# A decoder step on one core: the row blocks of the conditioning, one at a time or in twos

## The chip, the cores and the metric

One NeuronCore of a Trainium2 chip runs the whole program. The metric is the device time of one execution in microseconds. It was 1034.29 us for the kernel before (median of 3 runs, 1033.81 to 1036.57).

## The reference

One layer of a hybrid decoder over 512 prompt tokens and 8 single-token samples (520 columns together), width 1024, all in float32:

```python
cs = silu(c)                                   # 1 prompt and 8 sample vectors
mod = cs @ w_mod + b_mod                       # 9 x 6144: sh1, sc1, g1, sh2, sc2, g2
h = rmsnorm(x, norm1_g) * (1 + sc1) + sh1
u = h @ w_in                                   # q, f, i, o-gate; x, y; ga, gb (8 x 1024 columns)
o_a = HGRN2 recurrence of q, f, i, normed, times silu(o-gate)
o_b = RG-LRU recurrence of conv(x), times gelu(y)
merged = sigmoid(ga) * (o_a @ w_branch_a) + sigmoid(gb) * (o_b @ w_branch_b)
x = x + g1 * (merged @ w_out)
h2 = rmsnorm(x, norm2_g) * (1 + sc2) + sh2
x = x + g2 * (square(relu(h2 @ w_ff1)) @ w_ff2)
y = rmsnorm(x, final_norm_g)                   # and the new recurrent states
```

The change concerns the line `mod`. Its six parts of 1024 columns are numbered 0 to 5 (sh1, sc1, g1, sh2, sc2, g2). Parts 1 and 0 are computed at the start; parts 2, 4, 3 and 5, in this order, are computed in the tail of the mixer, between the tiles of other products.

## The kernel before, in words

Activations lie transposed, 128 features by 520 columns, in 8 slices. Every large product is made tile by tile: a weight tile of 1024 x 128 is loaded by SP into one of the four buffers `wst` (L102), split by ACT into a rounded high part `whi` (L111) and by DVE into the rest `wlo` (L114), and `gemm` runs 48 matmuls at L150: for each of 8 slices whi times the high and the low part of the activation and wlo times the high part, each in two halves of 260 columns. The results go to one of two PSUM tiles `mm`, and ACT or DVE reads them from there.

The conditioning is computed in **row blocks**: 128 rows of `w_mod` by the 1024 columns of one part, 512 KB, loaded by SP at L100 into the same four `wst` buffers, and used as they are. `mod_rows` (L408) runs four matmuls with the same 128 x 32 stationary tile `cT`, each for 256 columns and each into other 32 partitions of one PSUM tile `pt`. Eight row blocks make a part. Then ACT copies the sums out (`modev`, L413), and `mod_cols` (L422) transposes them by matmuls into `modT`; it is issued by the next `gemm` at its last slice (`MODK`).

The order of the work is a list of steps in `run`; each names the weights that it takes. In the tail it has the 8 tiles of gate ga, the 8 tiles of w_branch_a, then gate gb and w_branch_b tile by tile in turn, and then the 8 tiles of w_out and the MLP. `mod_step` puts the row blocks between them: one after each of the last four ga tiles, two after each of the first four w_branch_a tiles, one after each of the other four, and one after each of the 16 tiles of the last loop, 32 in all.

`weights` makes from the list the order of the loads. A row block gets the threshold of the tile before its step, a tile that of the tile two before it (`AHEAD`), and `ready_w` issues loads up to three entries (`LOADS`) ahead of the entry that is taken. A buffer of a tile is free when DVE has split it, a buffer of a row block when TensorE has read it. SP issues its transfers in order; one that waits for its buffer holds those behind it. At the beginning of the tail, POOL loads the results of both recurrences from DRAM, 16 slices in two tags of buffers (L877, L882), and ACT and DVE split them into `a` and `b` (L200, L201); x itself is loaded and transposed (L924, L927) for the output projection.

A scheduler with a model of the times then orders the instructions of each engine; it may set a few matmuls of one step between those of another.

Of the kernel before, what the change touches and what calls it, by code (L numbers as in the profile page):

```python
# [20 lines left out]
KO = D // 128  # L21
# [6 lines left out]
TAIL = 3  # L28
# [47 lines left out]
class Kernel:  # L76
# [355 lines left out]

    def mod(self, part, k):

        w = self.take_w(self.mod_key(part, k))
        if k == 0:
            self.psm = self.ppt.tile([128, 512], F32, name="pt")
        self.mod_rows(self.psm, k, w)
        if k == KO - 1:
            self.mod_open = part, self.modT[:, 8 * part:8 * part + 8], self.mod_out(self.psm), \  # L440
                self.n2g if part == 4 else None

# [1106 lines left out]
    def run(self):  # L1549
        tc, i, enter = self.tc, self.i, self.ctx.enter_context  # L1550
        self.consts = enter(tc.tile_pool(name="consts", bufs=1))
        self.dram = enter(tc.tile_pool(name="dram", bufs=1, space=DRAM))
        self.sm = enter(tc.tile_pool(name="sm", bufs=2))
        self.wst = enter(tc.tile_pool(name="wst", bufs=WST))
        self.ma = enter(tc.tile_pool(name="ma", bufs=8))
        self.ppt = enter(tc.tile_pool(name="ppt", bufs=1, space=PSUM))
        self.ppb = enter(tc.tile_pool(name="ppb", bufs=1, space=PSUM))
        self.pmm = enter(tc.tile_pool(name="pmm", bufs=2, space=PSUM))
        self.pps = enter(tc.tile_pool(name="pps", bufs=2, space=PSUM))
        self.whl = enter(tc.tile_pool(name="whl", bufs=2))  # L1560
        self.act = enter(tc.tile_pool(name="act", bufs=2))
        self.early = ExitStack()
        self.hc = self.early.enter_context(tc.tile_pool(name="hc", bufs=1))
        self.ogs = self.hc.tile([128, H, NB], F32, name="ogs")
        self.os = self.hc.tile([128, H, NB], F32, name="os")
        self.xlast = self.hc.tile([128, KO, 11], F32, name="xlast")
        self.hlast = self.hc.tile([128, KO, 9], F32, name="hlast")
        self.oaT_d = self.dram.tile([H, 128, L], F32, name="oaT_d")
        self.obT_d = self.dram.tile([KO, 128, T], F32, name="obT_d")
        self.oa, self.ob, self.merged = [], [], []  # L1570

        win = i["w_in"][0]
        steps = []
        one = lambda name, m, fn, *a: steps.append(([(i[name][0], 0, m * 128)], fn, *a))
        mods = [(p, k) for p in (2, 4, 3, 5) for k in range(KO)]

        def mod_step(n=1):
            for _ in range(n):
                if mods:
                    p, k = mods.pop(0)  # L1580
                    steps.append(([self.mod_key(p, k)], self.mod, p, k))

        ga, gb = {}, {}
        self.rg = {}

        for h in range(H):
            kf, kq, kv, kg = self.head_cols(h)
            steps.append(([kf, kq, kg, kv][FIRSTS if h == 0 else 0:], self.head_start if h == 0 else self.head, h))
            for n in (h - 1, h) if h % 2 else (h, h + 1):
                one("w_in", (40 if h % 2 else 32) + n, self.rg_y if h % 2 else self.rg_x, n)  # L1590
        for m in range(KO):
            one("w_in", 48 + m, lambda m: ga.update({m: self.gate(6, m, self.slot(self.ma, "ma"))}), m)
            if m == TAIL:
                steps.append(([], self.end_recurrences))
                steps.append(([], self.begin_tail))
            if m > TAIL:
                mod_step()
        for m in range(KO):
            if m == 2:
                steps.append(([], self.rg_out))  # L1600
            one("w_branch_a", m, lambda m: self.branch("w_branch_a", m, self.oa, ga[m]), m)
            mod_step(2 if m <= TAIL else 1)
        for m in range(KO):
            one("w_in", 56 + m, lambda m: gb.update({m: self.gate(7, m, self.slot(self.tail, "t"))}), m)
            mod_step()
            one("w_branch_b", m, lambda m: self.merge(m, gb.pop(m), ga.pop(m)), m)
            mod_step()
        steps.append(([], self.load_xT))
        steps.append(([], self.shifts))
        steps.append(([], self.begin_strassen))  # L1610
        for m in range(KO):
            one("w_out", m, self.out_proj, m)
        steps.append(([], self.norm2))
        self.entries, self.use = self.plan()
        steps.append((self.entries[:FIRST], self.mlp))

        keys = [k for st in steps for k in st[0]]
        self.mlp_at = len(keys) - FIRST
        self.weights(keys)
        self.begin()  # L1620
        for _, fn, *a in steps:
            fn(*a)
# [250 lines left out]
```

## Time and profile before

| what | value |
|---|---|
| timed runs, median (lowest to highest) | 1034.29 us (1033.81 to 1036.57) |
| profiled execution, first to last instruction | 1032.9 us |
| mean granted TensorE clock | 0.997 |
| PE busy, share of the span | 98% |
| DVE, ACT, POOL busy | 67%, 50%, 12% |
| HBM read, written | 123.61 MB, 11.26 MB |

The trace gives the start of each instruction from the span's start. For TensorE the starts are measured and the ends modelled, so costs between products are read from start to start. A matmul in float32 shows as two records. Idle time of an engine counts only where it delays the engine that sets the end. The tail's row blocks lie between 438.7 and 615.0 us.

### The profile page before, as it was taken

What the parts mean: (1) busy time and instruction counts of PE and PEld (TensorE: products, weight loads), DVE (VectorE), ACT (ScalarE), POOL (GpSimd) and SP (SyncE); (2) the same over time, 40 slices, a digit from 0 to 9 for tenths busy, and PEclk for the clock granted to TensorE, in tenths of its full rate; (3) what the DMA queues carried; (4) which work ended last, traced back from release to release, by engine and by line L of the source; (5) the groups of instructions that cost most, each with busy time, mean ns of one, the idle gap of its engine ahead of it and who ended that gap; (6) DMA issues with size and microseconds to landing.
All of it is one profiled execution on the core that took longest, in us unless ns stands there. A gap on an engine that the chain in (4) does not pass through costs nothing. (4 is left out here: it accounts for less than half of the span.)

```text
span 1032.9 us, 23726 instructions
## 1 busy us (share of the span) xinstructions
PE 1008.7 (98%) x9756; PEld 967.5 (94%) x9756; DVE 691.4 (67%) x1520; ACT 520.8 (50%) x988; POOL 123.1 (12%) x228
## 2 busy tenths in 40 slices
PE   5999999999999999999999999999999999999997
PEld 2899999999999999988999999999999999999996
DVE  6787769595867869264233347667776776777685
ACT  4555744663575366342122235466555655655663
POOL 3200000000000000031000001011422231232140
PEclk9999999999999999999999999999999999999998
DMA  9673443434334324397555568322672474274242
GB/s 324 220 200 111 119 126 118 121 116 126 109 114 126 114 85 135 105 329 238 164 163 162 158 179 240 99 84 63 133 173 81 95 173 124 49 160 99 63 82 84
DMA packets 201822, 143.68 MB, mean 139 GB/s; under 512 B 6766, under 2 KB 189702, under 8 KB 201706
## 3 DMA queue, kind: packets, MB, share of 16 engines
q1 hardware_dynamic: 191090, 128.08, 41.6%
q0 software_dynamic: 10608, 14.05, 7.0%
q8 instruction: 76, 1.25, 0.5%
q14 instruction: 32, 0.26, 0.1%
q10 hardware_dynamic: 16, 0.03, 0.0%
HBM read 123.61 MB, written 11.26 MB: 131 GB/s over the span
## 5 line engine op out<-in xcount | busy, mean ns | idle before, releaser
L150 PE MATMUL mm<-h,whi 128*128 128x260 f32 (+1 forms) x2944 | 490.3, 286 | 0.0
L150 PEld LDWEIGHTS mm<-h,whi 128*128 128x128 f32 x2944 | 409.7, 189 | 5.2 <-issue 4.1
L150 PE MATMUL mm<-h,wlo 128*128 128x260 f32 x1472 | 305.2, 286 | 0.1
L111 ACT CAST whi<-wst 128x1024 fp32r<-128x1024 f32 x164 | 171.7, 1048 | 221.6 <-PE mm L150 182.0
L114 DVE TENSOR_TENSOR wlo<-wst,whi 128x1024 fp32r<-128x1024 f32 x164 | 200.3, 1223 | 102.0 <-ACT whi L111 100.3
L150 PEld LDWEIGHTS mm<-h,wlo 128*128 128x128 f32 x1472 | 230.5, 189 | 1.9 <-issue 0.8
L150 PE MATMUL mm<-a,whi 128*128 128x260 f32 x512 | 85.3, 286 | 0.0
L150 PEld LDWEIGHTS mm<-a,whi 128*128 128x128 f32 x512 | 70.5, 188 | 3.8 <-issue 3.3
L150 PE MATMUL mm<-a,wlo 128*128 128x260 f32 x256 | 51.7, 283 | 0.0
L877 POOL DMA_DIRECT2D t<-oaT_d x8 | 4.4, 552 | 387.8 <-ACT sq L750 378.1
L1270 DVE TENSOR_TENSOR f<-f 128x260 f32<-128x260 f32 x64 | 27.4, 428 | 27.6 <-ACT f L1265 26.9
L1259 ACT ACTIVATE ft<-ft,fsh 128x512 f32<-128x512 f32 (+2 forms) x36 | 24.0, 675 | 36.1 <-DVE ft L1256 36.1
L150 PE MATMUL mm<-b,whi 128*128 128x260 f32 x256 | 41.9, 286 | 0.0
L1262 POOL TENSOR_TENSOR ft<-ft,fsh 128x8 f32<-128x8 f32 x28 | 18.4, 657 | 187.3 <-DVE ft L1256 187.3
L150 PEld LDWEIGHTS mm<-a,wlo 128*128 128x128 f32 x256 | 39.5, 188 | 0.0
L150 PEld LDWEIGHTS mm<-b,whi 128*128 128x128 f32 x256 | 35.0, 188 | 3.3 <-issue 2.5
L1304 POOL DMA_DIRECT2D ma<-snap x28 | 26.8, 972 | 38.3 <-issue 29.2
L1286 POOL DMA_DIRECT2D ma<-snap x28 | 25.9, 926 | 36.7 <-DMA ma<-snap 25.1
L893 DVE TENSOR_TENSOR t<-mm,t 128x520 f32<-128x520 f32 x8 | 5.6, 700 | 36.5 <-PE mm L150 36.5
L1265 ACT ACTIVATE f<-ft 128x520 f32<-128x520 f32 (+1 forms) x36 | 20.7, 587 | 15.0 <-POOL ft L1263 13.0
L602 ACT ACTIVATE st<-st,fkq 128x128 f32<-128x128 f32 x64 | 20.2, 391 | 14.8 <-DVE fkq L581 12.5
L150 PE MATMUL mm<-b,wlo 128*128 128x260 f32 x128 | 25.9, 284 | 0.0
(579 smaller groups left out, 1940.9 us busy)
## 6 DMA issues: line engine op xcount, KB each, us to landing
wst<-in_w_in_dram SPq DMA_DIRECT2D x64, 512.0 KB
wst<-in_w_mod_dram SPq DMA_DIRECT2D x32, 512.0 KB
wst<-in_w_ff_dram SPq DMA_DIRECT2D x64, 256.0 KB
wst<-in_w_ff_dram SPq DMA_DIRECT2D x32, 512.0 KB
wm<-in_w_mod_dram SPq DMA_DIRECT2D x16, 512.0 KB
st<-in_state_hgrn_dram SPq DMA_DIRECT2D x8, 512.0 KB
vb<-vd SPq DMA_DIRECT2D x8, 512.0 KB
out_dram<-st SPq DMA_DIRECT2D x8, 512.0 KB
```

What stands on the lines that cost most here:

```text
L111: ins = self.nc.scalar.copy(hi, st)
L114: self.nc.vector.tensor_tensor(lo, st, hi.bitcast(F32), OP.subtract)
L150: self.last_product = self.nc.tensor.matmul(ps[s][:, :c.stop - c.start], x, y[:, c], start=first and n == 0, stop=last and n == 2)
L602: nc.scalar.activation(st[:, b], st[:, b], AF.Copy, scale=fkq[:, 0, b:b + 1])
L877: nc.gpsimd.dma_start(t[:, :L], self.oaT_d[h])
L893: self.nc.vector.tensor_tensor(self.two(s), ps, self.two(s), OP.mult)
L1259: nc.scalar.activation(t[:, :p], t[:, :p], AF.Relu, bias=sh[:, 0:1])
L1262: eng.tensor_tensor(t[:, p:], t[:, p:], sh[:, 1:9], OP.add)
L1265: nc.scalar.activation(f, self.two(self.ft)[:, a:a + n], AF.Square)
L1270: self.nc.vector.tensor_tensor(f[:, n], f[:, a], f[:, b], op)
L1286: nc.gpsimd.dma_start(x[1][:, b], v[:, :n], accum_op=OP.add)
L1304: nc.gpsimd.dma_start(x[t][:, a], s[p], accum_op=OP.add)
```

## The change

The row blocks are taken two at a time. `mod` takes the weights of blocks k and k + 1 and runs both, one behind the other; the part is closed after block 6 and 7. `mod_step` adds one such step. The steps stand after the ga tiles 5 and 7, after the w_branch_a tiles 0 to 3, 5 and 7, and after each w_branch_b tile: 16 steps of two blocks. The work, the loads and their sizes are the same, and so are the buffers.

```diff
     def mod(self, part, k):
 
-        w = self.take_w(self.mod_key(part, k))
+        w = [self.take_w(self.mod_key(part, k + n)) for n in range(2)]
         if k == 0:
             self.psm = self.ppt.tile([128, 512], F32, name="pt")
-        self.mod_rows(self.psm, k, w)
-        if k == KO - 1:
+        for n in range(2):
+            self.mod_rows(self.psm, k + n, w[n])
+        if k == KO - 2:
             self.mod_open = part, self.modT[:, 8 * part:8 * part + 8], self.mod_out(self.psm), \
                 self.n2g if part == 4 else None
...
-        mods = [(p, k) for p in (2, 4, 3, 5) for k in range(KO)]
-
-        def mod_step(n=1):
-            for _ in range(n):
-                if mods:
-                    p, k = mods.pop(0)
-                    steps.append(([self.mod_key(p, k)], self.mod, p, k))
+        mods = [(p, k) for p in (2, 4, 3, 5) for k in range(0, KO, 2)]
+
+        def mod_step():
+            p, k = mods.pop(0)
+            steps.append(([self.mod_key(p, k + n) for n in range(2)], self.mod, p, k))
...
-            if m > TAIL:
+            if m > TAIL and m % 2:
                 mod_step()
         for m in range(KO):
             if m == 2:
                 steps.append(([], self.rg_out))
             one("w_branch_a", m, lambda m: self.branch("w_branch_a", m, self.oa, ga[m]), m)
-            mod_step(2 if m <= TAIL else 1)
+            if m <= TAIL or m % 2:
+                mod_step()
         for m in range(KO):
             one("w_in", 56 + m, lambda m: gb.update({m: self.gate(7, m, self.slot(self.tail, "t"))}), m)
-            mod_step()
             one("w_branch_b", m, lambda m: self.merge(m, gb.pop(m), ga.pop(m)), m)
             mod_step()
```

## The prediction

> **What bounds the kernel now.** I read the page's busy shares first, then the busy time by stretch, then the waits of TensorE, then TensorE's timeline around single row blocks, and last the timelines of SP and ACT where the loads are densest.
>
> ```profile
> span 1032.9 us, 23726 instructions
> PE 1008.7 (98%) x9756; PEld 967.5 (94%) x9756; DVE 691.4 (67%) x1520; ACT 520.8 (50%) x988; POOL 123.1 (12%) x228
> ...
> 443.00:474.00 31.00, 31.00 (x269) 27.32 (x268) 19.46 (x37) 14.70 (x23) 6.98 (x13) 1.00 1.00 332
> ...
> 485.00:615.00 130.00, 130.00 (x1123) 119.47 (x1121) 41.06 (x50) 29.41 (x38) 0.24 (x2) 1.00 0.57 166
> ...
> 660.00:1030.00 370.00, 365.20 (x3012) 364.22 (x3010) 266.33 (x450) 213.44 (x399) 88.95 (x151) 1.00 0.43 104
> ```
>
> In the last three rows the columns are the stretch, its length, then busy time of PE, PEld, DVE, ACT and POOL, the granted clock, the DMA share and GB/s. From 443 to 615 us, where every step of the change lies, PE is busy in every microsecond at full clock, and the view of TensorE's waits has no entry there. So the time of this stretch is the sum of what TensorE is given to do, and only what changes that sum, or what makes TensorE wait for the first time, can move the end. A busy PE is not a PE at its peak, though, so the next question is what one row block costs between two products.
>
> ```profile
> 445.76 0.41 PE L150 MATMUL mm<-h,wlo 128*128 128x260 f32 x2
> 446.10 0.64 PE L408 MATMUL pt<-wst,cT 128*32 128x256 f32 x8
> ...
> 447.25 0.40 PE L150 MATMUL mm<-h,wlo 128*128 128x260 f32 x2
> ...
> 452.30 0.40 PE L150 MATMUL mm<-h,wlo 128*128 128x260 f32 x2
> 452.63 0.64 PE L408 MATMUL pt<-wst,cT 128*32 128x256 f32 x8
> 453.20 0.75 PE L150 MATMUL mm<-a,whi 128*128 128x260 f32 x4
> ```
>
> A tile's product runs in eight groups of six matmuls, and each group ends with two wlo matmuls. From the wlo row at 447.25 to the one at 452.30 lie seven undisturbed groups: 5.05 / 7 = 0.721 us a group, so 5.77 us a tile. From 445.76 to 447.25 are 1.49 us with one row block inside (four matmuls, shown as 8 records). The block costs 1.49 - 0.72 = 0.77 us.
>
> ```profile
> 482.74 0.40 PE L150 MATMUL mm<-a,wlo 128*128 128x260 f32 x2
> 483.07 1.07 PE L408 MATMUL pt<-wst,cT 128*32 128x256 f32 x16
> ...
> 484.65 0.40 PE L150 MATMUL mm<-a,wlo 128*128 128x260 f32 x2
> ```
>
> Here the program of before already has two blocks back to back: 484.65 - 482.74 - 0.72 = 1.19 us. So a second block beside a first costs 0.42 us, not 0.77. The rest, 0.35 us, is the price of going from the products to the blocks' shape and back. This is the quantity the change buys.
>
> **The change part by part.** The blocks stay what they are; only their places move.
>
> ```profile
> L408 PE MATMUL pt<-wst,cT x256: 378/380/404, 438.7 to 615.0; 128*32 128x256 f32 x128
> ...
> 608.22 0.64 PE L408 MATMUL pt<-wst,cT 128*32 128x256 f32 x8
> ```
>
> There are 256 / 8 = 32 blocks. Walking TensorE's timeline of before, I find 8 of them in pairs already: the first two at 438.7 and those at 467.2, 476.1 and 483.1. Twenty stand alone, from 446.10 to 608.22; one is cut in two; two stand beside the transposition of a finished part (L422), at 516 and 569; and the last stands beside a transposition of x at 614.7. The order that the changed program gives TensorE has the same first two blocks and the same four existing pairs in place, and the other 24 blocks as 12 pairs: after the last gate tile of ga, after w_branch_a tiles 0, 5 and 7, and after each of the eight w_branch_b tiles. Thus before holds 20 singles, 1 cut, 2 beside L422, 1 beside x; after holds 11 plain pairs and 1 pair beside x.
>
> The cut block:
>
> ```profile
> 458.86 0.40 PE L150 MATMUL mm<-a,wlo 128*128 128x260 f32 x2
> ...
> 459.43 0.62 PE L408 MATMUL pt<-wst,cT 128*32 128x256 f32 x2
> ...
> 460.32 0.40 PE L150 MATMUL mm<-a,wlo 128*128 128x260 f32 x2
> 460.65 0.63 PE L408 MATMUL pt<-wst,cT 128*32 128x256 f32 x6
> ...
> 461.81 0.40 PE L150 MATMUL mm<-a,wlo 128*128 128x260 f32 x2
> ```
>
> Its parts cost 1.46 - 0.72 = 0.74 and 1.49 - 0.72 = 0.77, together 1.51 us: one block at the price of two.
>
> The transposition L422 is issued at the eighth group of the tile behind a part's last block. In before that is right ahead of the next block. In the new order no block follows the gate tiles, so twice, in the first and the fifth gate tile of gb, it stands alone:
>
> ```profile
> 515.78 0.41 PE L150 MATMUL mm<-h,wlo 128*128 128x260 f32 x2
> 516.02 0.53 PE L422 MATMUL pb<-ident,modev 128*128 128x36 f32 x4
> 516.48 0.64 PE L408 MATMUL pt<-wst,cT 128*32 128x256 f32 x8
> ...
> 517.63 0.40 PE L150 MATMUL mm<-b,wlo 128*128 128x260 f32 x2
> ...
> 648.81 0.40 PE L150 MATMUL mm<-a,wlo 128*128 128x260 f32 x2
> ...
> 649.29 0.53 PE L422 MATMUL pb<-ident,modev 128*128 128x36 f32 x4
> ...
> 649.98 0.40 PE L150 MATMUL mm<-a,wlo 128*128 128x260 f32 x2
> ```
>
> Beside a block the two together cost 1.85 - 0.72 = 1.13; alone L422 costs 1.17 - 0.72 = 0.45 us. The other two of the four L422 keep their neighbours.
>
> The sum: before 20 x 0.77 + 1.51 + 2 x 1.13 = 19.17 us, and the block beside x. After 11 x 1.19 + 2 x 0.45 = 13.99 us, and the pair beside x, which I price 0.42 over the single one. The gain is 19.17 - 13.99 - 0.42 = 4.76; as the rows carry two decimals and single blocks of the last loop come nearer to 0.765, I take 4.7 us.
>
> The Trainium skill, TensorEngine Tiling (Array Packing), Key Properties, says that a change of tiling mode drains the array. The 0.35 us row bears that out for blocks against products. But by that rule L422 (full columns) beside a block (32 columns) would be a change of mode too and share nothing with it, while the rows show 1.13 against 0.77 + 0.45 = 1.22; by the rule alone the two lone L422 would cost nothing extra and the gain would be 0.2 us larger. The measured 0.09 stands.
>
> What I cost at nothing, with its cover.
>
> ```profile
> wst<-in_w_mod_dram SPq DMA_DIRECT2D x32, 512.0 KB
> ```
>
> The loads on SP are reordered. Two row loads now stand together, and the second waits for the block that frees its buffer. In the last loop both row loads of a pair, and the branch tile behind them on SP, are issued when the pair before has run; that is two tiles, 11.5 us, ahead of their use. Three loads are 1.57 MB; at the 332 GB/s that the dense stretch reaches they take 4.7 us. Cover 6.8 us. The work of the other engines stays: the same splits run on ACT and DVE, one per tile. In the output projection the split of the third w_out tile goes behind that of a first w_ff2 half, whose load waits for the last pair; the tile is first read two tiles, 11.5 us, after that pair. POOL's queue is unchanged. After the last L422 TensorE's order is identical, so the gain is carried to the end, where PE is busy 365.2 of 370.0 us.
>
> The tight place is 443 to 474, where the DMA share is 1.00:
>
> ```profile
> 434.57 0.33 SPq L100 DMA_DIRECT2D wst<-in_w_mod_dram  x1
> 440.30 0.38 SPq L102 DMA_DIRECT2D wst<-in_w_branch_a_dram  x1
> ...
> 461.34 0.38 SPq L102 DMA_DIRECT2D wst<-in_w_branch_a_dram  x1
> ...
> 470.85 6.31 SPq L100 DMA_DIRECT2D wst<-in_w_mod_dram  x2
> ...
> 448.00 1.05 ACT L111 CAST whi<-wst 128x1024 fp32r<-128x1024 f32 x1 [2.96 <-DMA wst<-in_w_branch_a_dram]
> ...
> 468.52 1.05 ACT L111 CAST whi<-wst 128x1024 fp32r<-128x1024 f32 x1 [1.60 <-DMA wst<-in_w_branch_a_dram]
> ```
>
> Twice ACT waited for a tile that came 7.7 and 7.2 us after its issue. In the new order the first w_branch_a tile takes the place on SP of the row load at 434.57 and is issued some 6 us earlier, which removes the first of these waits. But the second row of the pair after w_branch_a tile 0 is issued only when the pair after ga has run. That pair ends at 452.63 - 0.77 + 1.19 = 453.05; the tile takes 5.77, half the pair 0.4: it is needed at 459.2, 6.1 us after its issue. If it takes the 7.2 to 7.7 us of the rows above, TensorE waits 1.1 to 1.6 us. A lower bound is the x2 row at 470.85: its second load was issued at its end, 477.16 less the issue of 0.33, and the block that reads it ran in the pair of 483.07 with no wait, so 6.2 us or less. I take 0, since the quick load is of the same kind (a row block released by a pair, ahead of a branch tile on SP), while the slow ones are weight tiles. The two ends, 0 and 1.6, go into the range. There is no second such loss behind it: the next pairs of w_branch_a tiles were pairs before and had the same lead.
>
> The profiled span is 1032.9 us, 1.4 under the median of the timed runs, 1034.29. What lies around the span does not change, so I subtract from the median: 1034.29 - 4.7 = 1029.6 us.
>
> **The rivals.** First, the rows come late in the dense stretch and eat part of the gain: 1.6 us at the pair after w_branch_a tile 0, and, as all later loads are pushed back by the burst, perhaps as much again at the next: 4.7 - 1.6 = 3.1 or 4.7 - 3.2 = 1.5, so 1031.2 to 1032.8. For it speaks the DMA share of 1.00, against it that ACT's two waits moved nothing on TensorE. The Trainium skill, DMA: Bandwidth & Descriptors, Queues, rings and completion order, says that a DMA engine takes its queues in turn, packet by packet. By that rule POOL's loads of the a and b tiles take half of the engines from SP's row loads here, which argues for this rival. No row of before shows the shares. I give it 0.20.
>
> Second, the gain is not kept: something later has a due time of its own, such as the loads of the MLP, and TensorE waits there by what it came earlier. Time 1034.3. Against it: DMA share 0.43 from 660 on, and loads on SP that are released by TensorE's and DVE's progress. 0.04. The same result would come if pairing did not save the switch, but the pair at 483.07 shows that it does.
>
> Third, slower: holding two of the four staging buffers for a pair turns the last loop into a burst and a pause, and at each of the eight w_branch_b pairs TensorE waits for the second row. It decides once three loads take longer than 11.5 us, that is under 137 GB/s. One microsecond at each pair is 8, net 1034.29 - 4.7 + 8 = 1037.6. The stretch moved 166 GB/s while only 0.57 busy, so the engines have twice what is needed: 0.05.
>
> **How the numbers follow.** The forecast has 0.71, the rivals 0.20, 0.04 and 0.05. A measurement of this kernel can tell about 0.3% from no change, 3.1 us, so faster means under 1031.2. The forecast is faster except for the scatter of the timed runs; half of the first rival's span lies near that line. Faster: 0.70 + 0.06 = 0.76. Within: 0.01 + 0.14 + 0.04 = 0.19. Slower: 0.05. The range reaches up through most of the first rival to 1032.3, and down to 1028.7, by the 0.2 of rounding, the 0.2 of L422 and half a microsecond of scatter.
>
> **What would show it.** In the timeline after, 16 groups of L408 with 16 records each, each costing 1.19 between the wlo rows; two lone L422 at 0.45; the other gate tiles of gb running straight into their w_branch_b tiles; no new entry among TensorE's waits; the last L408, at 615.0 in before by the row above, at about 610. A wait of PE on a w_mod load between 455 and 470 would be the first rival, one at every pair after 515 the third, and PE waits after 660 the second. The forecast is wrong if a pair still costs twice 0.77 in the new places.

## The result, and the profile after

The changed program took 1028.44 us (median of 5 runs, 1028.21 to 1029.88). The program before took 1034.54 us beside it (5 runs, 1033.81 to 1036.57). The ratio is 0.9942, interval 0.993 to 0.9955: faster by 0.6%. The forecast was 1029.6 us with a range from 1028.7 to 1032.3. The direction was right, and the time lies 0.26 us below the range.

The profiled execution took 1028.26 us, 1.76 more than its span. These are its busy shares and its stretches; the columns of the last three rows are those of the prediction's first fence, with the ends of the stretches moved to fit the new trace.

```profile
span 1026.5 us, 23725 instructions
...
PE 1004.4 (98%) x9756; PEld 967.8 (94%) x9756; DVE 691.1 (67%) x1520; ACT 520.4 (51%) x988; POOL 123.3 (12%) x228
...
441.00:472.00 31.00, 31.00 (x279) 28.12 (x279) 19.23 (x37) 14.38 (x23) 6.98 (x13) 1.00 0.99 328
483.00:608.00 125.00, 125.00 (x1101) 118.34 (x1103) 40.35 (x48) 29.50 (x38) 0.24 (x2) 1.00 0.55 167
658.00:1024.00 366.00, 360.77 (x2975) 359.78 (x2973) 262.77 (x443) 211.32 (x396) 88.98 (x151) 1.00 0.44 105
```

TensorE is as full as before in each of the three stretches, with the same number of instructions in all (9756) and 4.3 us less of busy time. The view of TensorE's waits from 440 to 660 us has no entry after the change. So nothing new waits there; there is less to do. The timeline of TensorE after, around the new pair after w_branch_a tile 0 and around a lone transposition L422, shows what each costs:

```profile
456.43 0.40 PE L150 MATMUL mm<-a,wlo 128*128 128x260 f32 x2
456.76 1.07 PE L408 MATMUL pt<-wst,cT 128*32 128x256 f32 x16
...
458.34 0.40 PE L150 MATMUL mm<-a,wlo 128*128 128x260 f32 x2
...
511.85 0.41 PE L150 MATMUL mm<-h,wlo 128*128 128x260 f32 x2
512.09 0.53 PE L422 MATMUL pb<-ident,modev 128*128 128x36 f32 x4
...
513.02 0.40 PE L150 MATMUL mm<-b,wlo 128*128 128x260 f32 x2
```

From wlo row to wlo row, less the 0.72 us of an undisturbed group, the pair costs 458.34 - 456.43 - 0.72 = 1.19 us (1.19 was taken), and the lone L422 costs 513.02 - 511.85 - 0.72 = 0.45 us (0.45 was taken).

**Where the 6.4 us of span went.** Two marks divide each trace: the first L408, and the first matmul of the second norm (ps<-sqs,ones_r), from which on both programs give TensorE the same order. The rows are those of before and then of after, from the answers on the tiles sqs and pt.

```profile
L973 PE MATMUL ps<-sqs,ones_r x4: 281/284/288, 673.6 to 674.6; 128*128 128x260 f32 x4
```

```profile
L408 PE MATMUL pt<-wst,cT x256: 379/379/403, 436.7 to 608.6; 128*32 128x256 f32 x128
...
L974 PE MATMUL ps<-sqs,ones_r x4: 280/283/288, 667.2 to 668.1; 128*128 128x260 f32 x4
```

The first L408 of before is at 438.7 (its row stands in the prediction). So 438.7 - 436.7 = 2.0 us had been won ahead of the change. Between the marks lie 673.6 - 438.7 = 234.9 us before and 667.2 - 436.7 = 230.5 after: 4.4 us. From the second mark to the end lie 359.3 us in both (1032.9 - 673.6 and 1026.5 - 667.2). The 4.4 is the change's; the 2.0 needs another cause. The last L408, which the prediction put at about 610, starts at 608.6. Most of it sits in one wait, near 253 us. These are the waits of TensorE from 240 to 440 us in before, and then VectorE and SP there; the instruction that follows in each row of VectorE needs a small tile that was written to DRAM (vd) and read back (vb).

```profile
PE ps L641 <- DVE X L687: 1.5, 1, 1.5
...
251.81 1.14 DVE L603 SCALAR_TENSOR_TENSOR st<-vb,fkq,st 128x128 f32<-128x128 f32 x4 [3.61 <-DMA vb<-vd]
...
243.96 0.30 SPq L593 DMA_DIRECT2D vd<-vs  x1
248.01 0.34 SPq L595 DMA_DIRECT2D vb<-vd  x1
```

The same rows of after:

```profile
249.54 1.14 DVE L604 SCALAR_TENSOR_TENSOR st<-vb,fkq,st 128x128 f32<-128x128 f32 x4 [1.69 <-DMA vb<-vd]
...
243.61 0.30 SPq L594 DMA_DIRECT2D vd<-vs  x1
245.85 0.34 SPq L596 DMA_DIRECT2D vb<-vd  x1
```

The write took 248.01 - 243.96 = 4.05 us until its read could be issued in before and 2.24 in after, VectorE waited 3.61 us instead of 1.69, and TensorE lost 1.5 us that it did not lose after. The code there is the same in both programs. (In a later trace, of pairs_but_last, the same write took 247.61 - 244.23 = 3.38 us, and TensorE waited 0.8 us at L641.)

### The profile page after: what moved, and what is told of

Same layout as the page of the kernel before. It is cut to its first block, busy times and chain, and to the rows that moved or that the text cites. A ratio compares the mean times of both kernels' runs of the same rounds, so it can differ in the third digit from the quotient of the medians.

```text
span 1026.5 us, 23725 instructions
## 1 busy us (share of the span) xinstructions
PE 1004.4 (98%) x9756; PEld 967.8 (94%) x9756; DVE 691.1 (67%) x1520; ACT 520.4 (51%) x988; POOL 123.3 (12%) x228
```

## The experiments

**The same two programs again.** Theory A calls the 2.0 us chance; theory B says that the change carries it.

> The kernel before, unchanged, timed against itself. In the first pair of traces the changed kernel reached its first row block of the tail at 436.7 us and the kernel before at 438.7, 2.0 us apart, although the change puts nothing ahead of that point; 1.6 us of it is one wait of TensorE at 253 us behind a slow write of a small tile to DRAM and back. Theory A (chance): these 2 us are scatter between executions; the first row block starts anywhere from 436.5 to 439 in any execution of either kernel, and a copy of the kernel before differs from it by 0.1% or less. Theory B (carried): something in the changed program shortens the part ahead of the tail each time; then this trace again shows the first row block at 438.7 within 0.3, with the wait at 253 us.

> The changed kernel, unchanged, in a second trace. The tail by its own rows should again gain 4.4 us on the kernel before (from the first row block to the last transposition of modT). Theory A: the first row block is not tied to 436.7; it may start up to 2 us later, and the time against before is 4.4 us less plus or minus what the heads scatter, 1028.5 to 1031. Theory B: it starts at 436.7 within 0.3 again and the time is 1028.4, 6 us less than before.

The program before took 1033.91 us (11 runs) beside 1034.11 of its own twin (27 runs): ratio 1.0001, 0.9992 to 1.001. The changed program took 1029.78 us (6 runs, 1029.21 to 1031.96): 0.9967, 0.9956 to 0.9979. The ratios here and below are estimates with their intervals; they are not the quotients of the two medians and differ from them by up to 0.001. Its second trace has the first L408 at 437.36. In the second trace of before, VectorE at the same place, the two marks, and TensorE's only wait between them read:

```profile
249.78 1.14 DVE L603 SCALAR_TENSOR_TENSOR st<-vb,fkq,st 128x128 f32<-128x128 f32 x4 [1.40 <-DMA vb<-vd]
...
436.83 0.63 PE L408 MATMUL pt<-wst,cT 128*32 128x256 f32 x4
...
PE pb L927 <- ACT ma L929: 0.6, 2, 0.3
...
L973 PE MATMUL ps<-sqs,ones_r x4: 280/283/288, 672.8 to 673.8; 128*128 128x260 f32 x4
```

The wait of 3.61 us is 1.40 here, and the program before reaches its first L408 at 436.83, as early as the changed one. Theory B falls: the 2.0 us were chance. In return this trace has 672.8 - 436.8 = 236.0 us between the marks, 1.1 more than the first. Two transpositions of x in the output projection (L927) wait for ACT there, whose copies L929 empty the tile pb. Ahead of them VectorE waits for half of a w_ff2 tile, and ACT for VectorE. That wait alone does not make the loss, though: the first trace of before has it too, and TensorE lost nothing there. The first two rows are of before_again, the last is of before:

```profile
631.35 0.69 DVE L1127 TENSOR_TENSOR wst<-wst 128x512 f32<-128x512 f32 x1 [3.27 <-DMA wst<-in_w_ff_dram]
...
636.90 0.66 PE L927 MATMUL pb<-ident,xin 128*128 128x128 f32 x4 [0.32 <-ACT ma L929]
...
632.20 0.69 DVE L1127 TENSOR_TENSOR wst<-wst 128x512 f32<-128x512 f32 x1 [3.40 <-DMA wst<-in_w_ff_dram]
```

The trace of after has 0.9 us for the wait of VectorE in place of 3.3, and a longer one of ACT for w_out, which the prediction had costed at nothing because the tile is read 11.5 us later. It cost TensorE no wait. The first row is of VectorE's waits, the second of ACT's, both after, from 600 to 660 us:

```profile
DVE wst L1128 <- DMA wst<-in_w_ff_dram: 0.9, 1, 0.9
...
ACT whi L111 <- DMA wst<-in_w_out_dram: 6.8, 2, 3.6
```

**Half of the change.** If each merging saves its 0.35 us and nothing else happens, the last loop and the places ahead of it must add up. In the variants that follow, `mod_step(n)` makes one step of n blocks, where in the program before it made n steps of one block.

```diff
 # pairs_last: blocks alone up to the last loop, pairs in it
             one("w_in", 56 + m, ...)
-            mod_step()
             one("w_branch_b", m, ...)
-            mod_step()
+            mod_step(2)
```

```diff
 # pairs_first: pairs ahead of the last loop, blocks alone in it
-            if m > TAIL:
-                mod_step()
+            if m > TAIL and m % 2:
+                mod_step(2)
...
-            mod_step(2 if m <= TAIL else 1)
+            if m <= TAIL or m % 2:
+                mod_step(2)
```

> Pairs only in the last loop (one after each w_branch_b tile); ahead of it the blocks stand as before. Same work. By the rows of the two traces, the last loop of before spends 13 x 0.766 + 2 x 1.133 + 1.160 = 13.4 us on blocks and transpositions beside them, in pairs 7 x 1.197 + 1.591 + 2 x 0.448 = 10.9: gain 2.5 us. Theory A: about 1032.0 for a before of 1034.5, with the scatter of the heads on top. Theory B with its cause in the last loop: 2.5 + 1.7, about 1030.3.

> Pairs only ahead of the last loop (after ga 5 and 7 and w_branch_a 0 to 3, 5 and 7); in the last loop one block after each tile as before. Same work. By the rows: 4.4 us of the whole less 2.5 of the last loop, 1.9 us gained, with the two w_branch_a blocks around the transposition of xlast costing 2.21 instead of 1.98. Theory A: about 1032.6. Theory B with its cause ahead of the last loop: 1.9 + 1.7, about 1030.9.

Timed, pairs_last took 1030.62 us (10 runs; 0.9974, 0.9965 to 0.9983) and pairs_first 1031.76 (11 runs; 0.9978, 0.9969 to 0.9986). In the traces, the stretch between the two marks is 232.39 us in pairs_last and 233.03 in pairs_first, against 234.89 in the first trace of before: gains of 2.50 and 1.86, together 4.36, which is the 4.4 of the whole. The two halves simply add. The timed medians give 1034.11 - 1030.62 = 3.5 and 1034.11 - 1031.76 = 2.35, together 5.8; the interval of pairs_last, 0.0017 to 0.0035 or 1.8 to 3.6 us, still holds the 2.5. By the ratios the gains are 2.7 and 2.3.

**The last pair alone.** The surplus raised theory C: pairing the last two blocks also removes the wait of VectorE for w_ff2 seen above, and with it an occasional loss of 1 us. Theory S says that it saves its switch and no more.

```diff
 # last_pair_only
-            mod_step()
+            if m < KO - 1:
+                mod_step()
             one("w_branch_b", m, ...)
-            mod_step()
+            mod_step(1 if m < KO - 1 else 2)
```

In pairs_but_last all but these two are paired: it has the steps of pairs_first ahead of the last loop and, in it, `mod_step(2 if m < KO - 1 else 1)` behind w_branch_b, with one `mod_step()` behind the last gate tile.

> The kernel before with one change: the two blocks after the last gate tile and the last w_branch_b tile stand together after the latter. Same work. In a second trace of the kernel before, TensorE lost 1.07 us in the output projection at two transpositions of x that waited for ACT, behind a DVE that waited 3.3 us for a w_ff2 half; traces with the last blocks paired show that DVE wait at 1 us and no loss. Theory S (switches alone): 0.764 + 1.160 - 1.591 = 0.33 us gained, ratio 0.9997. Theory C (the last pair also moves the order of loads and sums in the output projection, and with it a loss that strikes some executions): 0.3 to 1.4 us gained, ratio 0.9987 to 0.9997, with DVE's wait for w_ff2 near 1 us, ACT's wait for w_out near 6.6 us and no wait of TensorE there.

> The changed kernel with its last pair undone: one block after the last gate tile, one after the last w_branch_b tile. Same work. Theory S: 0.33 us slower than the changed kernel, that is 4.1 us faster than before (ratio 0.9960). Theory C: the out projection's order is that of before again, so DVE waits 3.3 us for the w_ff2 half and TensorE may lose up to 1.1 us at transpositions of x; ratio 0.9960 to 0.9972.

Beside 1034.16 us for before (15 runs), last_pair_only took 1033.05 (11 runs; 0.9989, 0.9981 to 0.9998) and pairs_but_last 1030.46 (5 runs; 0.9966, 0.9954 to 0.9979). The interval of last_pair_only, 0.2 to 2.0 us, holds both the 0.33 of S and the 1 of C. The traces say more. The stretch between the marks can be cut once more, at the first wlo row behind the last row block; what lies between the first mark and that row is the blocks' stretch, what comes behind it is the output projection. The row of before and then of after:

```profile
616.29 0.40 PE L150 MATMUL mm<-a,wlo 128*128 128x260 f32 x2
```

```profile
609.85 0.40 PE L150 MATMUL mm<-a,wlo 128*128 128x260 f32 x2
```

| trace | first L408 at, us | blocks' stretch, us | output projection to the second mark, us |
|---|---|---|---|
| before | 438.71 | 177.58 | 57.32 |
| before_again | 436.83 | 177.58 | 58.39 |
| last_pair_only | 437.46 | 177.24 | 57.58 |
| pairs_last | 436.91 | 175.07 | 57.32 |
| pairs_first | 436.77 | 175.70 | 57.33 |
| pairs_but_last | 438.14 | 173.52 | 57.33 |
| after | 436.66 | 173.19 | 57.30 |
| after_again | 437.36 | 173.19 | 57.47 |
| after_third | 436.81 | 173.53 | 57.52 |
| after_fourth | 438.36 | 173.19 | 57.45 |

In the blocks' stretch the change is worth 177.58 - 173.19 = 4.39 us, and three of its four traces show it to the hundredth (the fourth has a late row, told below). The halves are worth 2.51 and 1.88 there, and the last pair 0.34 by last_pair_only and 0.33 by pairs_but_last: that is theory S, though last_pair_only has most of it taken back in the output projection (57.58). The first column tells of chance again, for it starts anywhere from 436.66 to 438.71, with the changed program as with the others.

The waits that theory C named do move with the last pair: VectorE's longest wait for w_ff2 is 1.5 us in last_pair_only and 3.0 in pairs_but_last, and ACT waits 7.6 and 1.1 us in all for w_out. But pairs_but_last, like pairs_first and the first trace of before, has the long wait of VectorE and loses nothing in the output projection. Whether the loss of 1.1 us, seen in one of these four traces, happens more often without the last pair stays open, and so does the rest of the timed surplus.

**What exactly is saved.** Theory M takes the 0.35 us for the price of going from the full columns of the products to 32 columns and back; theory G takes it for the price of any gap between products. Here the tail's blocks use the 128 x 128 identity as the stationary tile instead of cT, so that parts 2 to 5 of the conditioning are not computed; the loads, the copies and the places stay those of before (wide_single) and of the changed program (wide_pairs).

```diff
+            x, out = (self.ident, ps[:, :256]) if wide else (self.cT[:, k, :], ps[32 * j:32 * j + 32, :256])
-            self.nc.tensor.matmul(ps[32 * j:32 * j + 32, :256], self.cT[:, k, :], w[:, 256 * j:256 * j + 256], ...)
+            self.nc.tensor.matmul(out, x, w[:, 256 * j:256 * j + 256], ...)
```

> Price of the switch by itself, first half. The order of before; each row block of the tail is multiplied by a full 128-column stationary tile (the identity) instead of the 32 columns of the conditioning, so the conditioning parts 2 to 5 are left out and other sums stand in their place. A block is then 4 matmuls x 2 passes x 256 columns that can't run side by side, about 8 x 0.118 = 0.95 us from the 0.120 us of a 260-column matmul. Theory M (the 0.34 us is a change between 128-column and 32-column tiling): no change of tiling any more, a lone block costs about 0.95. Theory G (any change from the products to float32 matmuls of another kind costs it): about 0.95 + 0.34 = 1.29.

> Second half: the changed kernel with the same full-width blocks (the same part of the computation is left out). Theory M: a pair costs twice a lone block of wide_single, 1.9 us, and pairing saves nothing. Theory G: a pair costs 0.34 less than two lone blocks, about 2.24 against 2 x 1.29.

One block in wide_single, and then one pair in wide_pairs, from TensorE's timelines:

```profile
523.60 0.41 PE L150 MATMUL mm<-a,wlo 128*128 128x260 f32 x2
523.84 1.89 PE L408 MATMUL pt<-wst,ident 128*128 128x256 f32 x8
...
526.04 0.40 PE L150 MATMUL mm<-h,wlo 128*128 128x260 f32 x2
```

```profile
519.97 0.41 PE L150 MATMUL mm<-a,wlo 128*128 128x260 f32 x2
520.21 3.62 PE L408 MATMUL pt<-wst,ident 128*128 128x256 f32 x16
...
524.14 0.40 PE L150 MATMUL mm<-h,wlo 128*128 128x260 f32 x2
```

A block costs 526.04 - 523.60 - 0.72 = 1.72 us and a pair 524.14 - 519.97 - 0.72 = 3.45, twice as much. Between the marks the two traces differ by 0.2 us (266.2 and 266.0), where theory G would have had about 12 x 0.35 = 4. Pairing full-width blocks saves nothing, so theory G falls and M stands: the change buys off changes of the array's shape, not gaps. Whether the time goes into emptying the array or into loading weights that then can't run ahead, these runs do not separate. The rule of the Trainium skill that the prediction weighed (TensorEngine Tiling (Array Packing), Key Properties), by which a change of the tiling mode drains the array, agrees with this; the rows give 0.35 us for going there and back. Expected was about 0.95 us for a wide block. It is 1.72. That the four matmuls do not run beside each other was already in the 0.95; what was wrong is the 0.118 us for a record, taken from the products' rows, where these take 1.72 / 8 = 0.215 each. Why was not followed; both theories are told apart by the pair against the single all the same. The times, one run each, were 1065.95 and 1063.9 us, and their first L408 are already 1.9 us apart (438.5 and 436.6), ahead of the first block that differs.

**Four at a time.** If pairs are good, one more step costs little: 8 steps of four blocks, after the last ga tile, after w_branch_a tiles 1, 4 and 7, and after every second w_branch_b tile. A step then holds all four staging buffers at once, and no branch tile can be loaded ahead of it.

```diff
-            if m > TAIL:
-                mod_step()
+            if m == KO - 1:
+                mod_step(4)
...
-            mod_step(2 if m <= TAIL else 1)
+            if m in (1, 4, 7):
+                mod_step(4)
...
-            mod_step()
             one("w_branch_b", m, ...)
-            mod_step()
+            if m % 2:
+                mod_step(4)
```

> Four blocks at a time in 8 steps (after ga 7, w_branch_a 1, 4, 7 and w_branch_b 1, 3, 5, 7), everything else as in the changed kernel. Same work. If only switches count, eight more of them go: 8 x 0.34 = 2.7 us faster than the changed kernel, about 1027. But four blocks hold all four staging buffers until the quad has run, and the next branch tile can then be loaded only 5.8 us ahead of its use, while a load takes 4 to 7 us and the split on ACT and DVE 2.3: a wait of 1 to 3 us at each of eight quads, 8 to 24 us. I expect 1032 to 1045, with TensorE waiting for the split of the tile after each quad.

> The changed kernel a third time, for the size of the gain: the first comparison gave 6.1 us between medians, the second 4.3. By the rows of the traces the switches are worth 4.4 us; with theory C, up to 1.1 more in the executions of before that lose it. Expected ratio 0.9945 to 0.9960, and in the trace again no wait of TensorE in the tail.

It took 1028.75 us (4 runs, 1027.38 to 1029.06; 0.9945, 0.9931 to 0.9958), with no stall of the size that was expected. The changed program took 1029.48 beside it (5 runs; 0.9958, 0.9944 to 0.9971). A step of four in the last loop in TensorE's timeline, the load and the split of the next w_branch_b tile in those of SP and ACT, and TensorE's waits from 425 to 670 us:

```profile
529.47 0.40 PE L150 MATMUL mm<-b,wlo 128*128 128x260 f32 x2
529.80 1.93 PE L408 MATMUL pt<-wst,cT 128*32 128x256 f32 x32
...
532.25 0.39 PE L150 MATMUL mm<-h,wlo 128*128 128x260 f32 x2
...
530.50 0.38 SPq L102 DMA_DIRECT2D wst<-in_w_branch_b_dram  x1
...
535.09 1.05 ACT L111 CAST whi<-wst 128x1024 fp32r<-128x1024 f32 x1 [3.02 <-DMA wst<-in_w_branch_b_dram]
...
PE mm L150 <- ACT whi L111: 0.4, 1, 0.4
PE mm L150 <- DVE wlo L114: 0.3, 1, 0.3
```

Four blocks cost 532.25 - 529.47 - 0.72 = 2.06 us; two pairs cost 2.39. That is one more excursion (from the products to the blocks and back) saved, and the waits are two small ones. The waits for loads on which the expectation rested are not there. It had the next tile issued only when all four blocks had run; SP issues it at 530.50, while they run, ACT has it 4.6 us later, and TensorE reads it at 537.53, 7.0 us after its issue.

The pair was run once more against the changed program:

> The kernel with four blocks at a time again, beside the changed kernel on the same chip. In its first trace the tail was 1.4 us shorter than the changed kernel's (248.4 against 249.8 between two fixed matmuls), of the 2.7 that the switches alone would give. Expected 1.0 to 1.6 us faster than the changed kernel, ratio to before 0.9935 to 0.9950. If the first result was chance: the same as the changed kernel.

> The changed kernel beside quads_again. If the switches are the whole of it, 4.4 us less than before, ratio 0.9957; the three comparisons so far gave 0.9942, 0.9967 and 0.9958.

Here quads_again took 1028.26 us (5 runs, 1027.35 to 1029.35; 0.9945, 0.9931 to 0.9958), after_fourth 1029.29 (5 runs; 0.9956, 0.9943 to 0.9969). Both times the fours are 0.7 to 1.0 us ahead, and both times the intervals overlap. The eight steps by themselves would save 8 x 0.33 = 2.6 us over sixteen pairs. The longest of TensorE's waits in quads_again over the same stretch shows where part of it goes:

```profile
PE pb L927 <- ACT ma L929: 0.9, 1, 0.9
```

The blocks' stretch, counted here from the row of the last transpositions of g (pt<-ident,g) ahead of the tail, takes 179.81 us in the trace of after, 178.09 in that of quads and 178.15 in that of quads_again: 1.7 us are won both times. That is less than 2.6; the step of four behind w_branch_a tile 1 is torn apart by the transpositions of xlast and hlast, and the rest was not followed. The output projection then takes 57.30, 57.64 and 59.16 us. In quads_again two transpositions of x cost 0.72 and 1.58 us there instead of 0.44, the second with the wait above, so the whole gain over the changed program is lost again in that trace. The version in fours beats the program before by 0.55% in both comparisons; that it beats the changed program by about 1 us is likely and not shown.

The trace of after_third shows one more thing, at the place that the first rival named. TensorE's timeline at the pair after w_branch_a tile 0, and the wait of its weight loads:

```profile
456.58 0.40 PE L150 MATMUL mm<-a,wlo 128*128 128x260 f32 x2
456.91 1.41 PE L408 MATMUL pt<-wst,cT 128*32 128x256 f32 x16
...
458.83 0.40 PE L150 MATMUL mm<-a,wlo 128*128 128x260 f32 x2
...
PEld pt L408 <- DMA wst<-in_w_mod_dram: 0.6, 1, 0.6
```

The pair costs 458.83 - 456.58 - 0.72 = 1.53 us instead of 1.19: the second row came late, by 0.34 us. In the first trace of after, and in those of after_again and after_fourth, this pair has no wait.

## Why the prediction was right and where it was wrong

**The unit costs were right.** A pair 1.19 us, L422 alone 0.45: both as forecast, and the blocks' stretch shrinks by the same 4.39 us in three traces of four. The price of the excursion has a cause that was only weighed before and is now shown, by the wide blocks.

**The sum was 0.3 us too large.** Forecast 4.7, found 4.4 between the marks. One term was missing, the edge of the pair at w_branch_a tile 1, which the prediction counted among "the same four existing pairs in place". The scheduler had laid that pair back to back ahead of the transpositions of xlast in before, and set six of them between its blocks in after. TensorE's timeline there, of before and then of after:

```profile
466.83 0.40 PE L150 MATMUL mm<-a,wlo 128*128 128x260 f32 x2
467.17 1.07 PE L408 MATMUL pt<-wst,cT 128*32 128x256 f32 x16
468.17 1.04 PE L865 MATMUL ps<-ident,xlast 128*11 128x128 f32 x8
...
469.54 0.40 PE L150 MATMUL mm<-a,wlo 128*128 128x260 f32 x2
```

```profile
463.37 0.40 PE L150 MATMUL mm<-a,wlo 128*128 128x260 f32 x2
463.70 0.64 PE L408 MATMUL pt<-wst,cT 128*32 128x256 f32 x8
464.27 0.82 PE L866 MATMUL ps<-ident,xlast 128*11 128x128 f32 x6
465.03 0.64 PE L408 MATMUL pt<-wst,cT 128*32 128x256 f32 x8
465.60 0.39 PE L866 MATMUL ps<-ident,xlast 128*11 128x128 f32 x2
...
466.31 0.40 PE L150 MATMUL mm<-a,wlo 128*128 128x260 f32 x2
```

The same 24 records cost 469.54 - 466.83 - 0.72 = 1.99 us before and 466.31 - 463.37 - 0.72 = 2.22 after: 0.23 lost. These transpositions have a stationary tile of 11 columns (128*11 in the rows), and still pay beside the 32-column blocks, so few columns alone do not give the blocks' shape. The other 0.1 is rounding: with single blocks at 0.765 and pairs at 1.195 the sum is 4.6.

**What was costed at nothing cost nothing.** The reordered loads of the last loop and the later split of the third w_out tile left no entry among TensorE's waits, though ACT waited 6.8 us for w_out tiles; in the three later traces of the changed program the output projection is up to 0.2 us longer. The removed wait of ACT in the dense stretch was replaced by a longer one (4.99 us for a w_branch_a tile, by its row at 460.11 in the trace of after), and that did not reach TensorE either.

**The rivals.** The first, rows late in the dense stretch, happened once in four traces of the changed program and took 0.34 us, not 1.6 to 3.2. The second and the third did not come: behind the second mark both first traces take 359.3 us, and the pairs of the last loop cost 1.20 us each in all four traces of the changed program, the last one, beside x, 1.59.

**The step that failed** is the lower end of the range, "half a microsecond of scatter", and behind it the subtraction of the gain from one median of before, which puts at nothing that the rest of the program takes different times in different executions. Two things were left out. First, what runs ahead of the row blocks does not take the same time in each execution: the first L408 lay 2.0 us apart in the first two traces, and anywhere from 436.66 to 438.71 us in the ten of the table. Behind 1.5 of the 2.0 us stands a write to DRAM that took 4.05 us in the one and 2.24 in the other trace of the same code. In line with that, 27 runs of before on one chip reached from 1032.79 to 1035.86 us. Second, the median of a few runs moves too. The changed program gave medians of 1028.44, 1029.78, 1029.48 and 1029.29 us in four series, 1.3 us from the lowest to the highest. With 1.3 in place of the 0.5 the range would have begun at 1027.9 and held the result.

The last three medians lie within 0.35 us of the forecast of 1029.6, but that is in part luck: the gain was 0.3 us too large, and the median that it was subtracted from, 1034.29, lay 0.1 to 0.3 above the later ones of before, so that the two errors cancel. Why the first series came out 0.9 to 1.3 us below the others stays open. A chip that is faster throughout does not explain it, as the program before had its highest median, 1034.54, beside it. The ratios of the four series, 0.9942, 0.9967, 0.9958 and 0.9956, have the mean 0.9956, or 4.6 us, close to the 4.4 of the traces. So the mechanism stands, and the scatter was taken too small.

## What to carry to other kernels

Where TensorE is full, look in its timeline for short groups in another tile shape between the products, and measure from product to product what one such excursion costs beyond its own matmuls; putting the groups side by side saves exactly that, and only if the shapes differ. Read the order of the changed program's instructions at every place that the change touches, also where it seems to leave them as they were: a scheduler may split what had stood together. When one forecasts a gain of half a per cent, the range needs the scatter of the medians, which is better taken from the spread of the runs shown (here 2.8 us for three runs) than guessed.

## What the runs showed of the hardware

Four matmuls with a 32-column stationary tile, each into other 32 partitions, take 0.42 to 0.43 us beside others of their kind (pairs and fours); with a 128-column one the same 256 columns each take 1.72 us, four times as much, alone or in a pair. Going from the products to the 32-column blocks and back costs 0.35 us; with 128-column blocks a pair (3.45 us) saved nothing against two single ones.

Transpositions between two 32-column blocks are not free either, even with a stationary tile of 11 columns: one more change there and back at xlast cost 0.23 us, about 0.12 each way, while L422 beside a block had saved only 0.09 us against standing alone.

A stall of VectorE by a DMA of one small tile, 1.40 and 3.61 us in two traces of one program, was followed by 1.5 us of waiting on TensorE in the second case, a third of what the change is worth.
